# First block tile of the FFN: weight sums on VectorE, operands split behind T1 in buffers of their own, T4 behind them, GpSimd's sums behind T4

## The chip, the cores and the metric

The kernel runs on one core of one Trainium2 chip. The metric is the device time of one execution in microseconds (us), lower is better; the median of three runs stands for a kernel. All matrix products run on TensorE (PE); VectorE (DVE) and ScalarE (ACT) cast, subtract and apply nonlinearities; GpSimd (POOL) does some elementwise sums; SyncE (SP) issues the DMAs.

## The reference, cut to what matters

One decoder block: a normalised input goes through three mixers, a gated merge and an output projection, and then through a SwiGLU feed-forward net (FFN). Only the FFN's input side matters here. D_MODEL is 1024, D_FF is 2816, 1024 tokens.

```
u = rms_norm(h, norm_ffn[l])
gate_ff, up_ff = jnp.split(u @ w_ffn_in[l], 2, axis=-1)
h = h + (jax.nn.silu(gate_ff) * up_ff) @ w_ffn_out[l]
```

## The kernel before

**Precision by splitting.** Each fp32 operand is split into a high part (an ACT copy rounded to the matmul's format, line 118) and a low part (a DVE subtraction, line 119); `split` at line 115 issues the two. A product of split operands takes three matmuls for each 128 rows of the contraction: hi by hi, hi by lo, lo by hi (`mm3`, line 143).

**The FFN's input side.** The 22 tiles f of 128 FFN channels each need gate and up columns of the weights. They are taken as pairs j and j + 11 for j = 0 to 10. The pair j = 0 is computed plainly: `swiglu_plain` (line 919) for f = 0 and f = 11, four groups of 24 matmuls each (banks mm_g and mm_u). Its weights come through the pool wp (tags wr, wh, wl, two buffers each). All others go through `swiglu` (line 943), a 2 by 2 block scheme with seven products of 12 matmuls in place of eight. The weight blocks are a11, a12 (gate, two halves of the contraction) and a21, a22 (up). Sums on GpSimd make a21 := a11 - a21, s2 := a22 - a21, later a11 := a11 + s2 and a12 := a12 - s2. The products follow in this order, with the PSUM banks that the profile shows: a11 by b11 (mm_s), a12 by b21 (sc_s), s2 by T2 (mm_s, added), a11 + s2 by T1 (tr_s), a21 by T3 (mm_s, added), a12 - s2 by b22 (tr_s, added), a22 by T4 (mm_s, added). Between them ACT and DVE read the banks: g0 (ACT copy, line 952, then a DVE add of sc_s), g1 (ACT copy of mm_s after the third product, line 960), u1 (ACT copy of tr_s after the fourth, line 963; DVE add of mm_s after the fifth, line 965). A product that is added into a bank waits for the read before it: the sixth waits for u1's copy, the seventh for u1's add.

**The weight operands.** `operand` (line 914) splits one 512-wide block into a tile [128, 2, 512]. In `swiglu` the first and sixth product take theirs from wp under the tag wh (two buffers), the second and seventh under wl (two), the other three from the pool r5 under the tag ar (three). In the tags wh and wl the plain part's last weights lie until its last matmuls.

**The token operands.** `combine` (line 976) makes T1 to T4 from the four blocks of the normalised tokens, once: 18 DVE sums and differences over 1024 elements a row and eight pairs of ACT copy and DVE subtraction, T2 and T3 first, then T1, then T4 (two of each, for the two halves of the contraction). T4's share is four sums and two pairs. T4's tiles take the buffers that b12 leaves when the plain part's last matmuls on it are done; the sums' temporaries take four buffers under the tag fo.

**Sums for the output side.** `combine_w(j)` (line 1006) loads two tiles of the FFN's output weights under the tag fo and forms four sums on GpSimd; `combine_a(j)` (line 1022) forms four more on GpSimd from the results of the pair j and j + 11. Both store what they make to DRAM (bsp and asp), and nothing reads that until the output side begins at about 1444 us.

**The order.** In the loop (line 1035) j = 0 runs `swiglu_plain` twice, `combine`, `combine_w(0)` and `combine_a(0)`; j = 1 then fetches its weights and runs `swiglu(1)`, `swiglu(12)`, and so on. `fetch_fi(f, i)` (line 934) loads the weights of the first of a pair into wp's wr and of the second into r5's wr. A planner places each instruction ahead of the run: it walks the program with costs of its own, gives each engine at each time the earliest instruction in the program that it takes to be ready, and the engines then work off these queues strictly in order. So a queue's order is the planner's expectation, and an instruction that is late holds up all behind it on its engine.

Of the kernel before, what the change touches and what calls it, by code (L numbers as in the profile page):

```python
# [11 lines left out]
AF = mybir.ActivationFunctionType  # L12
ALU = mybir.AluOpType
# [33 lines left out]
def f32(ap):  # L47
    return ap.bitcast(F32)
# [3 lines left out]
def hybrid_block(ctx, tc, h_in, w_in, w_v0, w_v1, w_bd, par, rows, gains, relt, onehot,  # L52
                 maskrow, cmask, w_br, w_out, w_fi, w_fo, out):
    nc = tc.nc
    act, dve, pool, pe = nc.scalar, nc.vector, nc.gpsimd, nc.tensor
# [11 lines left out]
    wp = ctx.enter_context(tc.tile_pool(name="wstream", bufs=2, side="left"))  # L67
# [26 lines left out]
    warm = cp.tile([P, 1], F32, name="warm")  # L94
# [20 lines left out]
    def split(hi, lo, src, scale=None, pin=False):  # L115

        if scale is None:
            act.activation(hi, src, AF.Copy)  # L118
            i = dve.tensor_tensor(lo, src, f32(hi), ALU.subtract)  # L119
            if pin:  # L120
                tc.keep_in_program_order(i)
        else:
            act.activation(hi, src, AF.Copy, scale=scale)
            dve.scalar_tensor_tensor(lo, src, scale, f32(hi), ALU.mult, ALU.subtract)

    def load_w(src, n, pl=None, tag="w", bufs=None, lo_on_pool=False):
        pl = pl or wp
# [149 lines left out]
    with tc.tile_pool(name="r0", bufs=1, side="right", reuse_waits="tile") as r0:  # L277
# [68 lines left out]
        bb = r0.tile([P, 8, 383], F32, name="bb")  # L346
# [417 lines left out]
    def pair_tile(pl, **kw):  # L764

        return [pl.tile([P, D], F32R, tag="m4", name=nm("pt"), **kw).rearrange("p (k t) -> p k t", k=2)
                for a in range(2)]
# [32 lines left out]
    with tc.tile_pool(name="r3", bufs=16, side="right", reuse_waits="tile") as r3:  # L800
# [13 lines left out]
        ahead = [fetch(*x, r3) for x in todo[:2]]  # L814
# [80 lines left out]
    NJ = NF // 2  # L895
# [3 lines left out]
    def sub(eng, o, a, b):  # L899
        eng.tensor_tensor(o, a, b, ALU.subtract)  # L900

    def add(eng, o, a, b):
        eng.tensor_tensor(o, a, b, ALU.add)

    with tc.tile_pool(name="r5", bufs=1, side="right", reuse_waits="tile") as r5:
# [3 lines left out]
        def product(ps, a, b, first=True):  # L909

            run(mm3(ps, [(a[:, 0, k * P:(k + 1) * P], a[:, 1, k * P:(k + 1) * P],
                          b[k // 2][0][:, k % 2], b[k // 2][1][:, k % 2]) for k in range(4)], first))

        def operand(pl, tag, bufs, src):
            t = pl.tile([P, 2, 512], F32R, tag=tag, bufs=bufs, name=nm(tag))
            split(t[:, 0], t[:, 1], src)
            return t
# [16 lines left out]
        def fetch_fi(f, i):  # L934
            w = []
            for s in range(2):
                pl = r5 if i % 2 else wp
                raw = pl.tile([P, D], F32, tag="wr", bufs=2, name=nm("wr"))
                dma(raw, w_fi[f + NF * s])
                w.append(halves(raw))  # L940
            return w

        def swiglu(f, w, bb):

            (a11, a12), (a21, a22) = w
            b11, b21, b22, t1, t2, t3, t4 = bb
            p1, p2, p5 = mm_bank(f"_s{f}"), sc_bank(f"_s{f}"), tr_bank(f"_s{f}")
            g0, g1, u1 = (t5("c", 6) for _ in range(3))
            s0, s1 = (t5("a", 6) for _ in range(2))
            s2 = t5("s2", 2)  # L950
            product(p1, operand(wp, "wh", 2, a11), b11)
            act.activation(g0, p1, AF.Copy)  # L952
            product(p2, operand(wp, "wl", 2, a12), b21)
            add(dve, g0, p2, g0)
            act.activation(s0, g0, AF.Sigmoid)
            dve.tensor_tensor(s0, g0, s0, ALU.mult)
            sub(pool, a21, a11, a21)
            sub(pool, s2, a22, a21)
            product(p1, operand(r5, "ar", 3, s2), t2, False)
            act.activation(g1, p1, AF.Copy)  # L960
            add(pool, a11, s2, a11)
            product(p5, operand(r5, "ar", 3, a11), t1)
            act.activation(u1, p5, AF.Copy)
            product(p1, operand(r5, "ar", 3, a21), t3, False)
            add(dve, u1, p1, u1)
            sub(pool, a12, a12, s2)
            product(p5, operand(wp, "wh", 2, a12), b22, False)
            add(dve, g1, p5, g1)
            act.activation(s1, g1, AF.Sigmoid)
            dve.tensor_tensor(s1, g1, s1, ALU.mult)  # L970
            dve.tensor_tensor(s1, u1, s1, ALU.mult)
            product(p1, operand(wp, "wl", 2, a22), t4, False)
            dve.tensor_tensor(s0, p1, s0, ALU.mult)
            return [s0, s1]

        def combine():

            b11, b21 = u2[0][:2], u2[0][2:]
            b12, b22 = u2[1][:2], u2[1][2:]
            t3 = [pair_tile(r5, bufs=4) for _ in range(2)]  # L980
            t2, t1 = ([pair_tile(mp) for _ in range(2)] for _ in range(2))
            temp = lambda: t5("fo", 4, D).rearrange("p (k t) -> p k t", k=2)
            v2 = []
            for i in range(2):
                v3 = temp()
                v2.append(temp())
                for v, x, y in zip((v3, v2[i]), b22[i], b12[i]):
                    sub(dve, v, f32(x), f32(y))
                add(dve, v3, v3, v2[i])
                for x, y in zip((v3, v2[i]), b11[i]):  # L990
                    add(dve, v2[i], x, f32(y))
                split(*t2[i], v2[i])
                split(*t3[i], v3)
            t4 = [pair_tile(mp) for _ in range(2)]
            for t, b in ((t1, b22), (t4, b21)):
                for i in range(2):
                    v = temp()
                    sub(dve, v, f32(b[i][0]), v2[i])
                    add(dve, v, v, f32(b[i][1]))
                    split(*t[i], v)  # L1000
            return b11, b21, b22, t1, t2, t3, t4

        def spill(i, j, x):
            dma(asp[i][j], x)

        def combine_w(j):

            raws = []
            for i in range(2):
                raw = t5("fo", 4, D)  # L1010
                dma(raw, w_fo[(j + NJ * i) * P:(j + NJ * i + 1) * P])
                raws += halves(raw)
            b11, b12, b21, b22 = raws
            t2 = zp.tile([P, 512], F32, tag="z", bufs=2, name=nm("t2"))
            sub(pool, b12, b22, b12)
            add(pool, t2, b12, b11)
            sub(pool, b11, b22, t2)
            sub(pool, b21, b21, t2)
            for i, x in ((2, t2), (3, b11), (4, b12), (6, b21)):
                dma(bsp[i][j], x)  # L1020
# [14 lines left out]
        for j in range(NJ):  # L1035
            if j == 0:
                first, second = swiglu_plain(0), swiglu_plain(NJ)
                bb = combine()
                spill(0, j, first[0])
            else:  # L1040
                first = swiglu(j, fetch_fi(j, 0), bb)
                spill(0, j, first[0])
                second = swiglu(j + NJ, fetch_fi(j + NJ, 1), bb)
            combine_w(j)
            combine_a(j, *first, *second)
    ctx4.close()


# [173 lines left out]
```

## Time and profile before

| | us |
|---|---|
| median of three runs | 1662.85 (1662.39 to 1664.62) |
| the profiled execution's own time | 1662.29 |
| its span, first to last instruction | 1660.5 |
| PE busy | 1630.2 (98%) |
| DVE busy | 999.4 (60%) |
| ACT busy | 760.7 (46%) |
| POOL busy | 433.1 (26%) |

The span is counted from the first instruction. Busy shares are averages over stages; what bounds a stage has to be read in that stage. PEclk is the granted TensorE clock, 1.00 for full speed. In the timeline a row is one engine's run of like instructions: start, length, what it does, and in brackets the idle time before it with what ended it.

### The profile page before, as it was taken

What the parts mean: (1) busy time and instruction counts of PE and PEld (TensorE: products, weight loads), DVE (VectorE), ACT (ScalarE), POOL (GpSimd) and SP (SyncE); (2) the same over time, 40 slices, a digit from 0 to 9 for tenths busy, and PEclk for the clock granted to TensorE, in tenths of its full rate; (3) what the DMA queues carried; (4) which work ended last, traced back from release to release, by engine and by line L of the source; (5) the groups of instructions that cost most, each with busy time, mean ns of one, the idle gap of its engine ahead of it and who ended that gap; (6) DMA issues with size and microseconds to landing.
All of it is one profiled execution on the core that took longest, in us unless ns stands there. A gap on an engine that the chain in (4) does not pass through costs nothing.

```text
span 1660.5 us, 22597 instructions
## 1 busy us (share of the span) xinstructions
PE 1630.2 (98%) x8159; PEld 1375.1 (83%) x8159; DVE 999.4 (60%) x1799; ACT 760.7 (46%) x1397; POOL 433.1 (26%) x341
## 2 busy tenths in 40 slices
PE   7999999999999999999999999899999999999998
PEld 6898978888888888888887888688888888888886
DVE  6565556555566666641348437977666676567544
ACT  6456466555555555542336434333333333345342
POOL 2111001001122221110225001776666566300000
PEclk9999999999999999999999999899999999999999
DMA  7132352223324142339737221464444443598642
GB/s 255 63 108 93 122 153 79 88 89 121 108 76 129 59 122 79 107 114 320 244 127 235 102 77 70 158 222 169 165 147 146 146 161 131 197 356 278 195 128 101
DMA packets 110879, 242.47 MB, mean 146 GB/s; under 512 B 11944, under 2 KB 23544, under 8 KB 110512
## 3 DMA queue, kind: packets, MB, share of 16 engines
q1 hardware_dynamic: 110768, 241.04, 42.7%
q8 instruction: 64, 1.05, 0.3%
q14 instruction: 47, 0.39, 0.1%
HBM read 163.45 MB, written 72.21 MB: 142 GB/s over the span
## 4 chain that ended last, share of the span: by engine, by line
PE 87%; DVE 4%; issue 4%; ACT 2%; POOL 1%; DMA 1%; SPq 0%; DVEq 0%; POOLq 0%; ACTq 0%
PE mm_w L150 26%; PE mm_s L150 13%; PE tr_s L150 7%; PE mm_br L150 6%; PE mm_wo L150 5%; PE mm_x L1086 4%; PE tr_y L1086 4%; PE sc_y L1086 4%; PE ob L547 3%; PE sc_s L150 3%; PE tr L558 3%; PE mm_v L150 2%; PE ob_x L1086 1%; PE mm_g L150 1%; PE mm_u L150 1%
## 5 line engine op out<-in xcount | busy, mean ns | idle before, releaser
L150 PE MATMUL mm_w<-uh,wh 128*128 128x512 f32 (+2 forms) x744 | 292.6, 393 | 0.0
L150 PE MATMUL mm_w<-uh,wl 128*128 128x512 f32 (+2 forms) x744 | 280.5, 377 | 0.0
L150 PE MATMUL mm_w<-ul,wh 128*128 128x512 f32 (+2 forms) x744 | 279.9, 376 | 0.0
L150 PEld LDWEIGHTS mm_w<-uh,wl 128*128 128x128 f32 x744 | 140.0, 188 | 25.7
L150 PEld LDWEIGHTS mm_w<-uh,wh 128*128 128x128 f32 x744 | 140.4, 189 | 12.7
L150 PEld LDWEIGHTS mm_w<-ul,wh 128*128 128x128 f32 x744 | 140.7, 189 | 11.7
L119 DVE TENSOR_TENSOR ab<-raw,ab 128x1024 fp32r<-128x1024 f32 x77 | 93.0, 1224 | 71.6 <-ACT ab L118 69.6
L118 ACT ACTIVATE ab<-raw 128x1024 fp32r<-128x1024 f32 x77 | 80.9, 1059 | 94.7 <-PE ob_x L1086 23.4
L150 PE MATMUL mm_s<-pt,ar 128*128 128x512 f32 x480 | 117.4, 394 | 3.7 <-ACT c L952 3.7
L118 ACT ACTIVATE wh<-wr 128x1024 fp32r<-128x1024 f32 (+1 forms) x85 | 72.7, 856 | 103.2 <-PE mm_w L150 50.6
L150 PE MATMUL mm_br<-o,wh 128*128 128x512 f32 x384 | 118.3, 389 | 0.0
L119 DVE TENSOR_TENSOR pl<-tr,ph 128x384 fp32r<-128x384 f32 (+2 forms) x160 | 87.4, 555 | 47.0 <-ACT ph L118 43.1
L150 PEld LDWEIGHTS mm_s<-pt,ar 128*128 128x128 f32 x480 | 91.5, 191 | 23.6 <-ACT c L952 4.5
L118 ACT ACTIVATE ph<-tr 128x384 fp32r<-128x384 f32 (+2 forms) x160 | 76.8, 485 | 53.6 <-PE tr L558 51.5
L119 DVE TENSOR_TENSOR wl<-wr,wh 128x1024 fp32r<-128x1024 f32 x45 | 55.6, 1235 | 72.2 <-ACT wh L118 71.9
L648 POOL TENSOR_SCALAR s<-s,sm 128x144 f32<-128x144 f32 (+3 forms) x64 | 48.6, 761 | 172.1 <-DVE sm L647 144.2
L150 PEld LDWEIGHTS mm_br<-o,wh 128*128 128x128 f32 x384 | 72.1, 188 | 14.9
L558 PE MATMUL tr<-ident,s 128*128 128x128 f32 x480 | 79.6, 274 | 1.2 <-POOL s L596 0.6
L150 PE MATMUL mm_wo<-woh,hl 128*128 128x512 f32 x256 | 79.1, 390 | 0.0
L150 PE MATMUL mm_br<-o,wl 128*128 128x512 f32 x192 | 75.3, 392 | 1.5 <-DVE wl L119 1.4
L558 PEld LDWEIGHTS tr<-ident,s 128*128 128x128 f32 x480 | 59.1, 140 | 18.3 <-DVE pl L119 3.4
L1086 PE MATMUL mm_x<-ab 128*128 128x512 f32 x297 | 72.7, 389 | 0.0
(252 smaller groups left out, 3687.9 us busy)
## 6 DMA issues: line engine op xcount, KB each, us to landing
wr<-w_in_dram SPq DMA_DIRECT2D x45, 512.0 KB, 3.7
wr<-w_fi_dram SPq DMA_DIRECT2D x44, 512.0 KB, 3.8
raw<-asp SPq DMA_DIRECT2D x77, 256.0 KB, 3.2
asp<-a SPq DMA_DIRECT2D x66, 256.0 KB, 2.5
gz<-z SPq DMA_DIRECT2D x48, 256.0 KB, 2.1
o<-osp SPq DMA_DIRECT2D x24, 512.0 KB, 6.1
sg<-gz SPq DMA_DIRECT2D x48, 256.0 KB, 3.2
fo<-w_fo_dram SPq DMA_DIRECT2D x22, 512.0 KB, 5.1
```

The costliest lines, as they stand in the source:

```text
L118: act.activation(hi, src, AF.Copy)
L119: i = dve.tensor_tensor(lo, src, f32(hi), ALU.subtract)
L150: pe.matmul(ps, a, b, start=first and i == 0, stop=i == n - 1, skip_group_check=not first)
L547: pe.matmul(ob[:, q0:q0 + b - a], vt[:, c], x[:, a:b], start=count == 0, stop=count == n_mm - 1, skip_group_check=True)
L558: pe.transpose(tb[:, col:col + P], src, ident)
L648: pool.tensor_scalar(s[:, :nk], s[:, :nk], den, 1.0, ALU.mult, ALU.mult)
L1086: pe.matmul(banks[x], a[:, 0, q], b[:, 1], start=first and j == 0 and c == 0, stop=j == NJ - 1 and c % 3 == 2, skip_group_check=True)
```

## The change

- `split` returns its two instructions.
- `fetch_fi` swaps the pools: the first of a pair goes to r5's wr, the second to wp's wr.
- `combine` stops after T1 and returns T1's last two split instructions (ACT's and DVE's) and a function `rest` that makes T4.
- At j = 0, behind `combine`, the weights of f = 1 are fetched and `swiglu(1)` is written there, with all of its ACT and DVE instructions queued behind T1's last split. In it a11, a12 and s2 are split first, into the three ar buffers; the sums a21 and s2 on DVE stand between; then T4 is made; then the products follow. All four weight sums of f = 1 are on DVE.
- A one-element GpSimd copy `seen` reads T4's last low part. The GpSimd instructions of `combine_w`, `combine_a` and of the second `swiglu` of each pair are queued behind it.
- For f = 12 (j = 1) the sums a21 and s2 are on DVE as well; its other two stay on GpSimd. All later tiles are as before.

```diff
         def fetch_fi(f, i):
...
-                pl = r5 if i % 2 else wp
+                pl = wp if i % 2 else r5
...
-        def swiglu(f, w, bb):
+        def swiglu(f, w, bb, eng, later=None):
...
+            def s32():
+                sub(eng[0], a21, a11, a21)
+                sub(eng[0], s2, a22, a21)
+
+            if later is None:
+                t4 = bb[6]
+                o1, o2 = (lambda: operand(wp, "wh", 2, a11)), (lambda: operand(wp, "wl", 2, a12))
+            else:
+
+                x1, x2 = (operand(r5, "ar", 3, a) for a in (a11, a12))
+                s32()
+                x3 = operand(r5, "ar", 3, s2)
+                t4 = later()
+                o1, o2 = (lambda: x1), (lambda: x2)
+            product(p1, o1(), b11)
...
-            sub(pool, a21, a11, a21)
-            sub(pool, s2, a22, a21)
-            product(p1, operand(r5, "ar", 3, s2), t2, False)
+            if later is None:
+                s32()
+                x3 = operand(r5, "ar", 3, s2)
+            product(p1, x3, t2, False)
...
-            add(pool, a11, s2, a11)
+            add(eng[1], a11, s2, a11)
...
-            sub(pool, a12, a12, s2)
+            sub(eng[1], a12, a12, s2)
...
+            last = less_t2(t1, b22)
+
+            def rest():
+                t4 = [pair_tile(mp) for _ in range(2)]
+                less_t2(t4, b21)
+                return t4
+            return [b11, b21, b22, t1, t2, t3], last, rest
...
-                bb = combine()
+                bb, last, rest = combine()
                 spill(0, j, first[0])
+                w = fetch_fi(1, 0)
+                with tc.issue_after(last[0]), tc.issue_after(last[1]):
+                    ahead = swiglu(1, w, bb, (dve, dve), lambda: bb.append(rest()) or bb[6])
+
+                seen = pool.tensor_copy(warm[:, 0:1], f32(bb[6][1][1][:, 0, :1]))
             else:
-                first = swiglu(j, fetch_fi(j, 0), bb)
+                first = ahead if j == 1 else swiglu(j, fetch_fi(j, 0), bb, (pool, pool))
                 spill(0, j, first[0])
-                second = swiglu(j + NJ, fetch_fi(j + NJ, 1), bb)
-            combine_w(j)
-            combine_a(j, *first, *second)
+                with tc.issue_after(seen.ins):
+                    second = swiglu(j + NJ, fetch_fi(j + NJ, 1), bb, (dve if j == 1 else pool, pool))
+            with tc.issue_after(seen.ins):
+                combine_w(j)
+                combine_a(j, *first, *second)
```

## Rows read from the trace of the kernel before

**Rows 1.** The page's share of busy time in 40 equal slices of the span (41.5 us each), in tenths.
```profile
PE   7999999999999999999999999899999999999998
DVE  6565556555566666641348437977666676567544
```
**Rows 2.** Busy time by stretch (columns: stretch in us, its length, then busy us and instructions of PE, PEld, DVE, ACT, POOL, then PEclk, DMA share, GB/s), from the start of the token sums to past the first block tile.
```profile
1013.00:1052.80 39.80, 39.80 (x177) 32.95 (x176) 39.11 (x39) 16.07 (x23) 14.27 (x5) 1.00 0.22 73
1052.80:1060.00 7.20, 4.28 (x18) 2.92 (x17) 7.20 (x7) 2.73 (x4) 5.43 (x3) 1.00 0.46 146
1060.00:1066.00 6.00, 2.94 (x9) 1.80 (x7) 4.37 (x4) 0.48 (x1) 5.92 (x5) 0.55 0.57 218
1066.00:1072.00 6.00, 5.32 (x15) 4.24 (x16) 5.82 (x5) 2.41 (x6) 5.29 (x4) 0.59 0.41 142
```
**Rows 3.** Timeline of PE over the first block tile, f = 1: the plain part's end and the products with b11, b21, T2, T1, T3.
```profile
1052.82 0.61 PE L150 MATMUL mm_s<-pt,wh 128*128 128x512 f32 x2
1054.33 2.56 PE L150 MATMUL mm_s<-pt,wh 128*128 128x512 f32 x10 [0.90 <-DVE wh L119]
...
1059.37 3.57 PE L150 MATMUL sc_s<-pt,wl 128*128 128x512 f32 x10 [2.02 <-DVE wl L119]
1066.68 4.96 PE L150 MATMUL mm_s<-pt,ar 128*128 128x512 f32 x12 [3.75 <-ACT c L952]
1071.48 2.88 PE L150 MATMUL tr_s<-pt,ar 128*128 128x512 f32 x12
1074.20 2.88 PE L150 MATMUL mm_s<-pt,ar 128*128 128x512 f32 x12
```
**Rows 4.** PE's waits from 1050 to 1440 us, all of them (columns: who waited for whom, total us, times, longest).
```profile
PE mm_s L150 <- ACT c L952: 3.7, 1, 3.7
PE sc_s L150 <- DVE wl L119: 2.0, 1, 2.0
PE mm_s L150 <- DVE wh L119: 0.9, 1, 0.9
```
**Rows 5.** The same columns as rows 2 in steps of 1 us: where the granted clock falls and where it rises again.
```profile
1060.00:1061.00 1.00, 1.00 (x5) 0.80 (x4) 1.00 (x2) 0.00 (x0) 0.92 (x2) 0.82 0.00 0
...
1070.00:1071.00 1.00, 1.00 (x4) 0.79 (x3) 1.00 (x2) 0.00 (x0) 0.37 (x2) 0.56 0.05 20
```
**Rows 6.** Timeline of ACT.
```profile
1048.66 0.64 ACT L118 ACTIVATE ar<-s 128x512 fp32r<-128x512 f32 x1 [9.69 <-POOL s L900]
...
1065.52 0.63 ACT L118 ACTIVATE wh<-wr 128x512 fp32r<-128x512 f32 x1 [7.25 <-POOL wr L900]
1066.05 0.58 ACT L952 ACTIVATE c<-mm_s 128x512 f32<-128x512 f32 x1
...
1072.28 0.62 ACT L118 ACTIVATE ar<-s 128x512 fp32r<-128x512 f32 x1
1074.40 0.60 ACT L963 ACTIVATE c<-tr_s 128x512 f32<-128x512 f32 x1 [1.50 <-PE tr_s L150]
```
**Rows 7.** Timeline of DVE: the token sums, T1 and T4, then the weights of f = 1 and f = 12 (an operation over 1024 elements a row is full width, over 512 half width).
```profile
1015.52 2.29 DVE L900 TENSOR_TENSOR fo<-pt,pt 128x1024 f32<-128x1024 f32 x1
...
1039.52 1.73 DVE L119 TENSOR_TENSOR pt<-fo,pt 128x1024 fp32r<-128x1024 f32 x1
1041.17 2.35 DVE L900 TENSOR_TENSOR fo<-pt,fo 128x1024 f32<-128x1024 f32 x2
...
1044.04 3.44 DVE L903 TENSOR_TENSOR fo<-fo,pt 128x1024 f32<-128x1024 f32 x2
1047.40 2.31 DVE L900 TENSOR_TENSOR fo<-pt,fo 128x1024 f32<-128x1024 f32 x1
1050.28 1.67 DVE L119 TENSOR_TENSOR pt<-fo,pt 128x1024 fp32r<-128x1024 f32 x1 [0.57 <-ACT pt L118]
...
1053.60 0.68 DVE L119 TENSOR_TENSOR wh<-wr,wh 128x512 fp32r<-128x512 f32 x1
...
1057.57 1.75 DVE L119 TENSOR_TENSOR wl<-wr,wl 128x512 fp32r<-128x512 f32 x1
...
1070.55 0.68 DVE L903 TENSOR_TENSOR c<-sc_s,c 128x512 f32<-128x512 f32 x1
...
1073.08 1.78 DVE L119 TENSOR_TENSOR ar<-s,ar 128x512 fp32r<-128x512 f32 x1
...
1077.12 0.69 DVE L903 TENSOR_TENSOR c<-mm_s,c 128x512 f32<-128x512 f32 x1 [0.56 <-PE mm_s L150]
```
**Rows 8.** Timeline of POOL: a sum with little beside it, then the first and the ninth of an almost unbroken run of sums (seven more lie between them).
```profile
1015.44 1.29 POOL L900 TENSOR_TENSOR wr<-wr,wr 128x512 f32<-128x512 f32 x1 [98.09 <-DVE pt L124]
...
1056.52 2.25 POOL L900 TENSOR_TENSOR fo<-fo,fo 128x512 f32<-128x512 f32 x1
...
1070.71 1.30 POOL L903 TENSOR_TENSOR wr<-s,wr 128x512 f32<-128x512 f32 x1 [0.63 <-DVE wh L119]
```
**Rows 9.** SP's queue: issues of DMAs in order.
```profile
1009.54 2.81 SPq L58 DMA_DIRECT2D wr<-w_fi_dram  x2
...
1040.19 0.33 SPq L58 DMA_DIRECT2D asp<-a  x1
1040.56 0.43 SPq L58 DMA_DIRECT2D wr<-w_fi_dram  x1
```

More of the change, by code (lines that the diff above doesn't have):

```diff
@@ L117, in split @@
         if scale is None:
-            act.activation(hi, src, AF.Copy)
+            a = act.activation(hi, src, AF.Copy)
             i = dve.tensor_tensor(lo, src, f32(hi), ALU.subtract)
@@ L122, in split @@
         else:
-            act.activation(hi, src, AF.Copy, scale=scale)
-            dve.scalar_tensor_tensor(lo, src, scale, f32(hi), ALU.mult, ALU.subtract)
+            a = act.activation(hi, src, AF.Copy, scale=scale)
+            i = dve.scalar_tensor_tensor(lo, src, scale, f32(hi), ALU.mult, ALU.subtract)
+        return a.ins, i.ins
     def load_w(src, n, pl=None, tag="w", bufs=None, lo_on_pool=False):
@@ L941, in fetch_fi @@
             return w
-        def swiglu(f, w, bb):
+        def swiglu(f, w, bb, eng, later=None):
             (a11, a12), (a21, a22) = w
-            b11, b21, b22, t1, t2, t3, t4 = bb
             p1, p2, p5 = mm_bank(f"_s{f}"), sc_bank(f"_s{f}"), tr_bank(f"_s{f}")
@@ L950, in swiglu @@
             s2 = t5("s2", 2)
-            product(p1, operand(wp, "wh", 2, a11), b11)
+            b11, b21, b22, t1, t2, t3 = bb[:6]
+            def s32():
[11 more added lines that the diff above has]
+            product(p1, o1(), b11)
             act.activation(g0, p1, AF.Copy)
-            product(p2, operand(wp, "wl", 2, a12), b21)
+            product(p2, o2(), b21)
             add(dve, g0, p2, g0)
@@ L993, in combine, with less_t2 @@
                 split(*t3[i], v3)
-            t4 = [pair_tile(mp) for _ in range(2)]
-            for t, b in ((t1, b22), (t4, b21)):
+            def less_t2(t, b):
                 for i in range(2):
@@ L999, in combine @@
                     add(dve, v, v, f32(b[i][1]))
-                    split(*t[i], v)
-            return b11, b21, b22, t1, t2, t3, t4
+                    last = split(*t[i], v)
+                return last
+            last = less_t2(t1, b22)
[4 more added lines that the diff above has]
+            return [b11, b21, b22, t1, t2, t3], last, rest
         def spill(i, j, x):
```

## The prediction

> **What bounds the kernel now.** First the page's slices of busy time: PE is at nine tenths or more in all but the first and last slices and one in the middle, around 1040 to 1080 us, and there DVE is at nine [rows 1]. So PE is the bound, and the one place where it loses time is where the FFN's token sums and first block tile fall. Then the stretches: up to 1052.8 PE is fully busy and DVE nearly so (39.11 of 39.80 us); in the next 13 us PE is busy for only 4.28 of 7.20 and 2.94 of 6.00 us, and the granted clock drops to about half [rows 2]. PE's timeline shows the loss. The plain part ends and the first product starts at 1052.82; a product takes 2.72 us from start to start (1071.48 to 1074.20), so T1's, the fourth, should start at 1052.82 + 3 x 2.72 = 1060.98. It starts at 1071.48 [rows 3]. **10.5 us** are lost, and no product after it is late: the list of waits holds 0.9, 2.0 and 3.7 us and nothing else until 1440 [rows 4]. The other 3.8 us are matmuls at the lower level, 1.2 GHz: the clock falls at about 1060.6, after the first two waits, and is back at 2.4 GHz at about 1070.9, some 4 us after work resumed [rows 5]; ten matmuls take 3.57 us and twelve 4.96 in place of 2.88 [rows 3]. The gain can't pass 10.5 us, 0.63%.
>
> Who is late? DVE splits a11 and a12 late (the first two waits), because T4 and the rest of the sums stand before them. The third wait is for ACT's g0 copy, and ACT stood 7.25 us behind a split that waited for a GpSimd sum [rows 6]. DVE is slow besides: a full-width operation, 1.22 us in an undisturbed run (2.35 for two), takes 2.31 while GpSimd sums run; a half-width one takes 0.68 alone and 1.75 to 1.78 beside GpSimd; one that reads PSUM stays at 0.68 there [rows 7].
>
> **The change part by part.** *T1 earlier.* T1's last low part ends at about 1051.9 now. Three of T4's operations before it go behind it: 3 x 1.13 (from start to start) = 3.4 us. GpSimd is silent until T4 is done, so these excesses go: 2.29 - 1.22, 1.73 - 1.22, 3.44 - 2.35, 2.31 - 1.22, 1.67 - 1.22 and the 0.57 of idling, together 4.8 [rows 7]. In their place DVE waits once for ACT's copy of T1's last sum, about 1.1. T1 ends at 1051.9 - 3.4 - 4.8 + 1.1 = 1044.8.
>
> *Operands and T4.* Then DVE does, alone, five half-width operations (low parts of a11, a12, s2, two sums) at 0.60 from start to start, two of the plain part's multiplications (1.2) and T4's six of 1.13: 3.0 + 1.2 + 6.8 = 11.0, so T4 ends at **1055.8**. The operands of the first three products are ready by about 1050, before PE needs them at 1052.82, even if T1 came 2 us late. They lie in ar, so they need no buffer of the plain part; T4 is first read by the seventh product, 16.3 us after 1052.82. The 0.9 and 2.0 us waits and the clock's first fall go, and I cost this part at nothing on the path.
>
> *Weights.* The tiles of f = 1 come into r5's buffers, whose loads are issued at 1009.54 now; wp's second load was issued at 1040.56, right behind a store of a GpSimd result [rows 9]. That store moves behind T4, so f = 12's loads, now in wp, no longer stand behind it. Nothing is lost.
>
> *GpSimd's queue.* Behind T4 stand `seen`, the four sums of `combine_w(0)`, the four of `combine_a(0)` and then f = 12's remaining two. Now they begin at 1056.52 and eight take 1070.71 - 0.63 - 1056.52 = 13.6 us, 1.70 each [rows 8]. They begin about when they do now, at 1057, so the eight end at 1070.6, while PE is 10.5 us ahead. Their stores on SP move with them, and the loads behind these (f = 2's weights, 13 us or more ahead of need) have slack.
>
> *What is late next.* DVE takes over six sums, 0.60 each. From 1055.8 its queue holds, ahead of f = 12's s2 becoming ready: two sums and two low parts for a11 and a12, low parts of a22 and a21, two operations for the gate, two low parts of f = 12, its sums a21 and s2, twelve in all, 12 x 0.60 = 7.2. GpSimd's eight sums fall into just this time. In rows 7, from 1057.57 to the one at 1073.08, ten half-width operations from SBUF take 14.8 us, 1.48 each or 0.8 more than 0.68, beside about ten GpSimd sums. So 8 x 0.8 = 6.4 us come on top: s2 of f = 12 is ready at 1055.8 + 7.2 + 6.4 = 1069.4. The planner, which counts no such excess (it let ACT run into that 7.25 us wait), expects it at about 1063 and will put its ACT copy ahead of u1's, as it stands now (1072.28 before 1074.40 [rows 6]). So u1's copy ends at 1069.4 + 0.62 + 0.60 = 1070.6, and the sixth product, due at 1052.82 + 5 x 2.72 = 1066.42, waits **4.2 us**. A wait of that size is likely to bring the lower clock back: the bounds are nothing and the whole 3.3 us of its present cost (1.2 and 2.1 by rows 3); I take the 2.1 of the one full product, being the nearest case of work after a long wait. The same backlog holds u1's add in DVE's queue, where f = 12's low parts stand before it as now (1073.08 before 1077.12), which this wait covers.
>
> Sum: 10.5 - 4.2 - 2.1 = **4.2 us** gained. The profiled execution's 1662.29 (span 1660.5 and 1.8 around it) would become 1658.1; it lies 0.6 below the median, so the median becomes 1662.85 - 4.2 = **1658.7**. Bounds of the excess for one GpSimd sum: nothing gives no wait (1652.4); 1.1, the most that rows 7 show (1.78 - 0.68), gives 8.8 in place of 6.4, a wait of 6.6 and with the clock's 3.3 a gain of 0.6 (1662.3).
>
> **The rivals.** *No new stall.* If the planner puts f = 12's DVE and ACT work behind u1's copy and add, or the excess is small, PE runs through: 1662.85 - 10.5 = 1652.4. For it: since 1074 the same engines serve PE without a wait, with GpSimd beside them. Against it: the orders named above.
>
> *Full exclusion.* If each GpSimd sum holds DVE off for its whole 1.29 us [rows 8], eight cost 10.3: s2 at 1073.3, the sixth product at 1074.5, a wait of 8.1 and 2.1 for the clock, a gain of 0.3: 1662.6. Against it, no row shows over 1.1. This is the Trainium skill's rule (SBUF — State Buffer, section "Who interferes with whom"): the two engines share a port pair under an exclusive lock, and a VectorE operation with two SBUF inputs contends with GpSimd's reads. The rule speaks against gathering GpSimd's sums where DVE has most to do; the trace agrees in kind (0.68 for PSUM sources, up to 1.78 for SBUF) but shows less than a whole sum's length.
>
> *Slower: GpSimd's queue.* f = 12's sum a11 + s2 stands in GpSimd's queue behind whatever the planner thought ready first. If it expects the eight sums done before s2, it puts sums of `combine_w(1)` in the gap. With four of them a11 + s2 ends at 1070.6 + 5 x 1.70 = 1079.1; its ACT copy and low part stand before u1's add (0.62 + 0.69 + 0.69), so the seventh product, due at 1069.14, starts at 1081.1: 12.0 lost, 14.1 with the clock, 3.6 more than now: 1666.4. It turns from gain to loss at two such sums. For it: the planner takes GpSimd to be faster than it is; against it: those sums need their own load first.
>
> **How the numbers follow.** Forecast 0.45; no new stall 0.22; full exclusion 0.17; slower 0.16. What a measurement can tell from no change is 0.2%, 3.3 us. The forecast's own range, 1653 to 1662.3, puts about 0.30 of its 0.45 beyond that; with the 0.22 faster has 0.52. Full exclusion, the forecast's rest and the slower case with two or three sums make 0.36 the same; 0.12 is left for slower. The range 1652.2 to 1664.5 leaves out the slower case's upper part.
>
> **What would show it.** Right: the first five products 2.72 us apart from about 1052.8; T4's last low part near 1056 and GpSimd's first sum just after; one PE wait of 3 to 7 us at f = 1's sixth or seventh product, released by ACT's u1 copy or DVE's add, with an ACT copy of s2 (or of a11) just before it; PEclk near 0.5 in the products after it; f = 12 without waits. Wrong: PE late for x1 or x2 (T1 later than I work out), no wait at all, or a wait after f = 1, where I expect none because GpSimd catches up in its idle time.

## The result and the profile after

| | before | after |
|---|---|---|
| median, us (11 runs each, same chip) | 1662.39 (1660.84 to 1664.62) | 1665.34 (1664.79 to 1667.67) |
| ratio, 95% interval | | 1.002 (1.0012 to 1.0028) |
| profiled execution, us | 1662.29 | 1667.67 |
| its span, us | 1660.5 | 1665.9 |
| f = 1's first product starts, us | 1052.82 | 1054.13 |
| from there to the start of f = 12's second product | 32.26 | 36.20 |

The change makes the kernel slower by 2.95 us, 0.18%; the interval lies wholly on the slow side. The time lies outside the range of the prediction.

Of the 5.4 us between the two profiled executions, 1.3 lie ahead of f = 1: the plain part ends later. In the fourteen executions profiled for this study f = 1 starts anywhere between 1051.65 and 1054.66 us, behind the same plain part, so this 1.3 is taken as scatter and not as an effect of the change. From f = 1's first product to f = 12's second, eight products lie; at 2.72 us each they need 21.76 us. Before they took 32.26, that is 10.5 lost; now they take 36.20, **14.4 lost**. The difference is 3.9 us, inside the interval of the ratio (2.0 to 4.7 us).

The two views that tell where: first the waits of PE in the profile after, between 1000 and 1440 us (columns as in [rows 4]). The three of before are gone, and two others are there.

```profile
PE mm_s L151 <- DVE c L904: 4.9, 1, 4.9
PE tr_s L151 <- ACT c L980: 3.7, 1, 3.7
```

Then PE's timeline after, from f = 1's first product on (it answers to [rows 3]):

```profile
1054.13 2.88 PE L151 MATMUL mm_s<-pt,ar 128*128 128x512 f32 x12
1056.85 2.88 PE L151 MATMUL sc_s<-pt,ar 128*128 128x512 f32 x12
...
1065.01 2.88 PE L151 MATMUL mm_s<-pt,ar 128*128 128x512 f32 x12
1071.54 5.49 PE L151 MATMUL tr_s<-pt,wh 128*128 128x512 f32 x12 [3.65 <-ACT c L980]
1081.91 5.49 PE L151 MATMUL mm_s<-pt,wl 128*128 128x512 f32 x12 [4.87 <-DVE c L904]
1087.19 3.30 PE L151 MATMUL mm_s<-pt,wh 128*128 128x512 f32 x12
1090.33 2.88 PE L151 MATMUL sc_s<-pt,wl 128*128 128x512 f32 x12
```

The first five products stand 2.72 us apart: what the change was to remove, it removed. Then the sixth waits 3.65 us for u1's copy (ACT, line 980), and the seventh another 4.87 us for u1's add (DVE, line 904). Each of the two takes 5.49 us in place of 2.88, and the one after them 3.30. Waits 8.5, matmuls at the lower clock 2.6 + 2.6 + 0.4 = 5.6: that is the 14.4, to 0.3 (a wait is counted from the end of the product before it, 0.16 after the next one could have started).

Who is late for the sixth? Timeline of DVE after, from T4's last part on (compare [rows 7]):

```profile
1056.47 0.68 DVE L904 TENSOR_TENSOR wr<-s,wr 128x512 f32<-128x512 f32 x1
1057.07 0.69 DVE L901 TENSOR_TENSOR wr<-wr,s 128x512 f32<-128x512 f32 x1
1057.68 1.23 DVE L119 TENSOR_TENSOR pt<-fo,pt 128x1024 fp32r<-128x1024 f32 x1
...
1061.74 1.78 DVE L119 TENSOR_TENSOR wl<-wr,wl 128x512 fp32r<-128x512 f32 x1
1063.44 1.77 DVE L972 TENSOR_TENSOR a<-c,a 128x512 f32<-128x512 f32 x1
1065.14 1.78 DVE L119 TENSOR_TENSOR wh<-wr,wh 128x512 fp32r<-128x512 f32 x1
...
1068.54 1.75 DVE L901 TENSOR_TENSOR s<-wr 128x512 f32<-128x512 f32 x1
1071.04 0.92 DVE L119 TENSOR_TENSOR ar<-s,ar 128x512 fp32r<-128x512 f32 x1 [0.76 <-ACT ar L118]
1080.17 1.08 DVE L119 TENSOR_TENSOR ar<-wr,ar 128x512 fp32r<-128x512 f32 x1 [8.21 <-ACT ar L118]
1081.18 0.68 DVE L904 TENSOR_TENSOR c<-mm_s,c 128x512 f32<-128x512 f32 x1
```

T4 is done at 1058.9. Up to there a half-width operation takes 0.68; beside GpSimd's sums it takes 1.75 to 1.78, 1.70 from start to start. So f = 12's s2 (1068.54) is ready at 1070.3 only. Two lines of ACT's timeline after show what hangs on it, and a third on what the seventh's wait hangs:

```profile
1070.38 0.63 ACT L118 ACTIVATE ar<-s 128x512 fp32r<-128x512 f32 x1 [7.29 <-DVE s L901]
1070.91 0.58 ACT L980 ACTIVATE c<-tr_s 128x512 f32<-128x512 f32 x1
1079.51 1.15 ACT L118 ACTIVATE ar<-wr 128x512 fp32r<-128x512 f32 x2 [8.02 <-POOL wr L904]
```

ACT idles 7.29 us before its copy of s2, which DVE has not made yet; u1's copy is next in its queue, though the fourth product, which it reads, ended at 1065.2. Later ACT idles 8.02 us before its copy of f = 12's a11 + s2, which GpSimd (POOL) has not made. DVE idles 8.21 us for that copy, to make its low part; u1's add, for which PE waits, comes after it, though u1's copy was done at 1071.5. POOL's timeline after shows why a11 + s2 is late:

```profile
1059.51 1.76 POOL L901 TENSOR_TENSOR fo<-fo,fo 128x512 f32<-128x512 f32 x1
...
1071.37 1.72 POOL L901 TENSOR_TENSOR a<-a,t 128x512 f32<-128x512 f32 x1
1073.05 1.27 POOL L901 TENSOR_TENSOR fo<-fo,fo 128x512 f32<-128x512 f32 x1
1074.40 1.28 POOL L904 TENSOR_TENSOR t<-fo 128x512 f32<-128x512 f32 x1
1075.76 2.50 POOL L901 TENSOR_TENSOR fo<-fo,t 128x512 f32<-128x512 f32 x2
1078.21 1.26 POOL L904 TENSOR_TENSOR wr<-s,wr 128x512 f32<-128x512 f32 x1
```

The eight sums of j = 0, which like those of `combine_w(1)` have no haste (nothing reads them before the output side), fill it from 1059.51 to 1073.05. Then come the four of `combine_w(1)` (1073.05 to 1078.21, the one with x2 is two), and only then a11 + s2, done at 1079.5. Its source s2 was there from 1070.3, so it could have begun at 1073.05.

Last, stretches of the profile after (columns as in [rows 2]): PE's clock.

```profile
1072.00:1074.00 2.00, 2.00 (x6) 1.54 (x6) 0.00 (x0) 0.00 (x0) 2.00 (x2) 0.50 0.70 270
1082.00:1084.00 2.00, 2.00 (x5) 1.61 (x6) 1.90 (x4) 0.63 (x1) 0.00 (x0) 0.50 0.46 182
1088.00:1089.00 1.00, 1.00 (x6) 0.80 (x5) 0.79 (x2) 0.06 (x1) 0.80 (x1) 1.00 0.03 10
```

After each of the two waits the granted clock is 0.50, that is 1.2 GHz, though PE is busy throughout; at 1088 it is back at 1.00.

### The profile page after: what moved, and what is told of

Its sections match the earlier page's. It is cut to its first block, busy times and chain, and to the rows that moved or that the text cites. A ratio compares the mean times of both kernels' runs of the same rounds, so it can differ in the third digit from the quotient of the medians.

```text
span 1665.9 us, 22589 instructions
## 1 busy us (share of the span) xinstructions
PE 1632.4 (98%) x8159; PEld 1376.9 (83%) x8159; DVE 993.3 (60%) x1805; ACT 761.4 (46%) x1397; POOL 415.3 (25%) x336
## 4 chain that ended last, share of the span: by engine, by line
PE 84%; DVE 5%; issue 4%; ACT 2%; DMA 2%; POOL 2%; SPq 0%; DVEq 0%; POOLq 0%; ACTq 0%
PE mm_w L151 24%; PE mm_s L151 13%; PE tr_s L151 6%; PE mm_br L151 6%; PE mm_wo L151 5%; PE mm_x L1118 4%; PE tr_y L1118 4%; PE sc_y L1118 4%; PE ob L548 3%; PE sc_s L151 3%; PE tr L559 3%; PE mm_v L151 2%; PE ob_x L1118 1%; PE mm_g L151 1%; PE sc L633 1%
```

## The experiments

The theory after the result: GpSimd's sums, gathered behind T4, make DVE late (first wait) and then keep f = 12's a11 + s2 behind sums that have no haste (second wait); the orders of ACT's and DVE's queues pass both on to PE. The rivals: that DVE is simply overloaded by the sums it took over; that the waits would only move when the order is mended. Every edit below is one to the changed kernel. Since the start of f = 1 scatters by 3 us, the table also has the time from f = 1's first product to the end, as the profiled execution's time less that product's start.

| kernel | median, us (runs) | ratio to before, interval | profiled: f = 1 to the end |
|---|---|---|---|
| before | 1662.39 (11) | | 609.5 |
| the change | 1665.34 (11) | 1.002 (1.0012 to 1.0028) | 613.5 |
| e1_w1_behind | 1659.21 (11) | 0.9983 (0.9975 to 0.9992) | 606.9 |
| e2_f12_dve | 1659.22 (11) | 0.9981 (0.9972 to 0.999) | 606.3 |
| e3_u1_first | 1658.74 (11) | 0.9976 (0.9967 to 0.9985) | 606.5 |
| e6_both | 1658.28 (11) | 0.9976 (0.9967 to 0.9984) | 606.5 |
| e4_no_sums0 | 1652.03 (5) | 0.994 (0.9928 to 0.9953) | 599.0 |
| e5_no_seen | 1660.3 (11) | 0.999 (0.9981 to 0.9999) | 607.3 |
| e8_hold | 1663.84 (11) | 1.0008 (0.9999 to 1.0017) | 611.0 |
| e9_f12_first | 1659.89 (11) | 0.9986 (0.9977 to 0.9995) | 607.1 |
| e7_f12_pool | 1663.4 (10) | 1.0007 (0.9998 to 1.0016) | 610.3 |
| e10_w_later | 1656.8 (5) | 0.9964 (0.9951 to 0.9976) | 602.9 |
| e11_w_later2 | 1668.6 (5) | 1.0037 (1.0024 to 1.0051) | 613.8 |
| e12_w_catch_up | 1657.78 (7) | 0.9972 (0.9961 to 0.9983) | 604.2 |

Each ratio is to runs of before taken beside that kernel on the same chip; their medians lie between 1662.18 and 1662.85, and "below before" means below these. The change was not run again beside the experiments, so a difference to its 1665.34 is one between chips and carries that scatter of some 0.7 us.

**The sums of j = 1 behind f = 12's** (e1_w1_behind). `add` and `sub` return their instruction here and below.

```diff
-            sub(eng[1], a12, a12, s2)
+            tail[f] = sub(eng[1], a12, a12, s2).ins
...
-            with tc.issue_after(seen.ins):
+            with tc.issue_after(tail[NJ + 1] if j == 1 else seen.ins):
                 combine_w(j)
                 combine_a(j, *first, *second)
```

> The changed kernel, but the GpSimd sums of j = 1 (combine_w(1), combine_a(1)) are queued behind f = 12's last weight sum, so its a11 + s2 stands ninth behind T4 and not thirteenth. Theory (GpSimd's queue makes the second wait): a11 + s2 ends at about 1074.4 in place of 1079.5, its ACT copy and low part by 1075.7, u1's add by 1076.4, before the sixth product ends at about 1077; the wait of 4.9 us before the seventh product goes, the 3.7 us before the sixth stays. 4.9 to 7.5 us under the changed kernel (the upper end if the clock is back at 2.4 GHz for the seventh product): 1657.8 to 1660.5. Rival (DVE has too much work in this stretch, by the sums moved to it): u1's add is as late as before, both waits stay, 1665.

Measured 1659.21, as the theory had it: 6.1 below the change. PE's timeline of this kernel, sixth and seventh product:

```profile
1071.79 5.48 PE L151 MATMUL tr_s<-pt,wh 128*128 128x512 f32 x12 [3.65 <-ACT c L980]
1077.08 3.00 PE L151 MATMUL mm_s<-pt,wl 128*128 128x512 f32 x12
```

The sixth's wait stays at 3.65, the seventh's is gone, and with it the second fall of the clock. So four sums without haste, ahead of f = 12's a11 + s2 in GpSimd's queue, make the second wait, and all of it.

**All of f = 12's sums on DVE** (e2_f12_dve).

```diff
-                    second = swiglu(j + NJ, fetch_fi(j + NJ, 1), bb, (dve if j == 1 else pool, pool))
+                    second = swiglu(j + NJ, fetch_fi(j + NJ, 1), bb, (dve, dve) if j == 1 else (pool, pool))
```

> The changed kernel, but all four weight sums of f = 12 are on DVE, two more there. Theory (GpSimd's queue makes the second wait): a11 + s2 follows s2 on DVE at about 1070.3, u1's add is done by 1074 to 1075, the wait before the seventh product goes, the one before the sixth stays at 3 to 5 us: 1657.5 to 1660.5. Rival (too much work on DVE): two more operations of up to 1.78 us each make both waits longer, 1666 to 1669.

Measured 1659.22. The first wait is 3.6; of the second 1.5 are left, behind sums that DVE now makes itself. It agrees with e1 on the place: two sums more on DVE are cheaper than two behind GpSimd's backlog, so DVE's own load is not the cause of the second wait.

**u1's copy and add ahead of f = 12's late work** (e3_u1_first). f = 12's sums a21 and s2 and the splits of s2 and a11 + s2 are queued behind f = 1's u1 copy and add.

```diff
+            if f == NJ + 1:
+                for x in u1s[1]:
+                    behind.enter_context(tc.issue_after(x))
...
-            act.activation(u1, p5, AF.Copy)
+            u1s[f] = [act.activation(u1, p5, AF.Copy).ins]
```

> The changed kernel, but f = 12's sums a21 and s2 and the splits of s2 and a11 + s2 are queued behind f = 1's u1 copy on ACT and u1 add on DVE. GpSimd's order stays. Theory (both waits are the work of f = 12 standing ahead of f = 1's in strictly ordered queues): no wait in f = 1. GpSimd's a11 + s2 still ends near 1079.5, and ACT's copy of it now stands ahead of f = 12's g0 copy, so f = 12's third product, due near 1078.6, waits 3 to 4 us, with some 2 us for the clock: 1656.5 to 1659. Rival (the buffers: the three ar tiles taken by the early operands hold up the later ones whatever the order): waits stay in f = 1, 1662 or more.

Measured 1658.74. Both waits of f = 1 are gone; one came back in f = 12, at its third product, in PE's list of waits of this kernel:

```profile
PE mm_s L151 <- ACT c L968: 4.4, 1, 4.4
```

It is the size expected (3 to 4), 0.4 over. Line 968 is g0's copy: ACT is again behind a split whose source is late. So the orders pass the lateness on, and mending them at one place moves it.

**Both** (e6_both): the edits of e1 and e3 together.

> e3's order on ACT and DVE and e1's on GpSimd together. Theory: f = 12's s2 is split by about 1073.5 and a11 + s2 by about 1076, before PE needs them (1078.6 and 1081.3), and f = 1 runs through, so PE has no wait after 1054: all of the changed kernel's 14 us of waits and low clock go, 1651 to 1652.5, which is 10 to 11 us under the kernel before. Rival (too much work on DVE and GpSimd in this stretch, whatever the order): the waits come back in f = 12, 1657 or more.

Measured 1658.28: a miss by 6 us, and the rival was right. Three views of this kernel, PE, ACT and DVE:

```profile
1086.47 5.49 PE L151 MATMUL mm_s<-pt,ar 128*128 128x512 f32 x12 [4.27 <-ACT c L982]
```

```profile
1085.31 0.63 ACT L971 ACTIVATE a<-c 128x512 f32<-128x512 f32 x1 [7.87 <-DVE c L904]
1085.84 0.58 ACT L982 ACTIVATE c<-mm_s 128x512 f32<-128x512 f32 x1
```

```profile
1082.93 1.75 DVE L119 TENSOR_TENSOR wh<-wr,wh 128x512 fp32r<-128x512 f32 x1
1084.60 0.68 DVE L904 TENSOR_TENSOR c<-sc_s,c 128x512 f32<-128x512 f32 x1
```

The wait stands two products further, at f = 12's fifth. ACT waits 7.87 us for g0's add, which DVE reaches only at 1084.60, with operations of 1.75 us ahead of it. DVE is still late, because GpSimd is still at its sums.

**Without the eight sums of j = 0** (e4_no_sums0). This is the test of the root: what `combine_w(0)` and `combine_a(0)` store is stored unsummed, so the kernel leaves out that part of the FFN's result. Their loads and stores stay.

```diff
-            sub(pool, b12, b22, b12)
...
+            if j == 0:
+                t2 = b22
+            else:
+                sub(pool, b12, b22, b12)
...
+            if j == 0:
+                s2 = a22
+            else:
+                sub(pool, a21, a11, a21)
```

> The changed kernel without the eight GpSimd sums of j = 0: combine_w(0) and combine_a(0) store their inputs as they are in place of the sums (that part of the FFN's result is left out). DVE's and ACT's work stays. Theory (GpSimd's sums slow DVE): f = 12's half-width operations on DVE take 0.68 us in place of 1.75, its s2 is ready near 1064 in place of 1070.3, and GpSimd has nothing ahead of a11 + s2: neither wait of the changed kernel is left, 1651 to 1653. Rival (DVE has too much work there by the six sums moved to it): the wait before the sixth product stays at 2 us or more, and the clock's loss with it, 1656 or more.

Measured 1652.03, 10.2 us below before, within the theory's range. PE's list of waits is empty from 1000 to 1440. In DVE's timeline of this kernel the operations that took 1.75 to 1.78 are back at 0.68:

```profile
1061.72 0.68 DVE L119 TENSOR_TENSOR wh<-wr,wh 128x512 fp32r<-128x512 f32 x1
...
1062.92 0.68 DVE L901 TENSOR_TENSOR s<-wr 128x512 f32<-128x512 f32 x1
```

From f = 1 to the end it takes 599.0 us: the 609.5 of before less the 10.5 that before loses there. So DVE with all six moved sums is in time, s2 is ready at 1063.6 in place of 1070.3, and both waits hang on the eight sums of GpSimd. The rival of a DVE overloaded by what it took over falls, and so does one that the trace would also allow, that DVE is slowed by the transfers beside it: from 1060 to 1064, where its operations take 0.68 here, the DMA engines move 356 GB/s, and in the change, where they take 1.75 to 1.78 (1060.6 to 1070.3), 122.

**Without the hold** (e5_no_seen): `seen` and the queueing behind it are left out, so GpSimd may begin ahead of T4's end.

```diff
-                seen = pool.tensor_copy(warm[:, 0:1], f32(bb[6][1][1][:, 0, :1]))
...
-            with tc.issue_after(seen.ins):
+            if True:
```

> The changed kernel without its last part: GpSimd's sums are not held behind T4 (no copy seen). In GpSimd's queue f = 12's a11 + s2 then stands behind the eight sums of j = 0 and ahead of those of j = 1. Theory: the sums start some 3 us earlier and slow T4 a little, which has slack; the wait before the seventh product goes, the one before the sixth stays at 2 to 4 us: 1656.5 to 1660. Rival (holding GpSimd back is what keeps T4 and the first operands in time): a wait before the first or the seventh product by T4, 1662 or more.

Measured 1660.3, 5.0 below the change and 0.3 over the theory's upper end. PE waits 0.9 at the fifth product and 4.4 at the sixth, and not at the seventh. In POOL's timeline f = 12's a11 + s2 now stands ahead of the sums of j = 1:

```profile
1067.48 1.71 POOL L901 TENSOR_TENSOR a<-a,t 128x512 f32<-128x512 f32 x1
1071.07 1.27 POOL L904 TENSOR_TENSOR wr<-s,wr 128x512 f32<-128x512 f32 x1 [1.88 <-issue]
```

So the part of the change that holds GpSimd behind T4 costs 5 us by itself: without it one of the eight sums is done before 1035 and the other seven begin at 1056.88, the order in the queue is another, and the second wait does not come.

**GpSimd held a second time** (e8_hold): e6, and all later GpSimd work held until f = 12's g0 is there.

```diff
+            if j == 1:
+                with tc.issue_after(tail[NJ + 1]):
+                    seen = pool.tensor_copy(warm[:, 0:1], gs[NJ + 1][:, :1])
```

> e6 (f = 12's work behind f = 1's u1, GpSimd's sums of j = 1 behind f = 12's), and the GpSimd sums of j = 1 and of f = 2 are held back further, behind a small copy that reads f = 12's g0 after its add. Theory (DVE is only slow beside GpSimd): between f = 12's last GpSimd sum and g0's add DVE's half-width operations take 0.68 us in place of 1.75, g0's add is done near 1077 in place of 1085 and the wait that e6 has left (4.3 us before f = 12's fifth product) goes: 1651 to 1653. Rival (there is more work than the engines can do here; a wait only moves): the wait comes up again in f = 12 or in f = 2, 1656 or more.

Measured 1663.84, a miss by 11 us. e6's wait is gone, as meant, but PE and ACT of this kernel show the next one:

```profile
1090.98 4.71 PE L151 MATMUL tr_s<-pt,wh 128*128 128x512 f32 x12 [5.25 <-ACT c L991]
...
1117.52 4.61 PE L151 MATMUL mm_s<-pt,wl 128*128 128x512 f32 x12 [2.79 <-DVE c L904]
```

```profile
1089.81 0.63 ACT L118 ACTIVATE ar<-s 128x512 fp32r<-128x512 f32 x1 [8.62 <-POOL s L901]
```

The products with brackets are f = 12's sixth and f = 2's seventh. Now the sums of f = 2, which are GpSimd's, are late: ACT waits 8.62 for f = 2's s2, and f = 12's u1 copy, for which the sixth waits, is next in its queue. The time in which GpSimd is kept still is missing afterwards. The wait of 2.79 is of the same kind as the change's second: f = 2's u1 add stands on DVE behind the low part of f = 13's a11 + s2, which GpSimd makes only from 1113.81 to 1115.09.

**f = 12's two sums first** (e9_f12_first): behind T4 first f = 12's two, then the sums of j = 0 and j = 1.

```diff
+            if j == 0:
+                first0, second0 = first, second
+                continue
+            with tc.issue_after(tail[NJ + 1]):
+                if j == 1:
+                    combine_w(0)
+                    combine_a(0, *first0, *second0)
```

> The changed kernel, with f = 12's two GpSimd sums first behind T4 and the sums of j = 0, then of j = 1, behind them. GpSimd then has nothing to do until f = 12's s2 is ready on DVE. Theory (GpSimd beside DVE, and GpSimd's order): s2 is ready near 1064, a11 + s2 near 1065.5, no wait in f = 1; the eight sums then fall beside f = 1's end and f = 12, where at most 1 to 3 us of wait come up: 1651.5 to 1656. Rival (the same amount of contention, only moved, costs the same): waits of 4 us or more in f = 12, with the clock, 1657 or more.

Measured 1659.89, above the theory's range and in the rival's. No product of f = 1 waits, and f = 12's s2 is ready at 1063.6 as in e4, though the eight sums are only moved here. f = 12's seventh waits:

```profile
1093.77 4.60 PE L151 MATMUL mm_s<-pt,wl 128*128 128x512 f32 x12 [4.80 <-DVE c L904]
```

ACT stands 5.52 us behind f = 2's a11 + s2 (1090.08 to 1091.34 on GpSimd), which has the eight, five sums of j = 1 and f = 2's own two ahead of it: the wait is the change's second one, one tile later. f = 2's seventh waits another 1.0.

**f = 12's a21 and s2 back on GpSimd** (e7_f12_pool).

```diff
-                    second = swiglu(j + NJ, fetch_fi(j + NJ, 1), bb, (dve if j == 1 else pool, pool))
+                    second = swiglu(j + NJ, fetch_fi(j + NJ, 1), bb, (pool, pool))
```

> The changed kernel with f = 12's sums a21 and s2 back on GpSimd; the rest of the change stays. Theory: s2 stands behind the eight sums of j = 0 and one of j = 1 in GpSimd's queue and ends near 1076 in place of 1070.3, so the wait before the sixth product grows from 3.7 to 9 us or so; a11 + s2 follows two sums later, near 1079, so the wait before the seventh product shrinks to 1 to 3 us: 1664 to 1669. Rival (the sums moved to DVE are what costs): without them the wait before the sixth product shrinks, 1661 or less.

Measured 1663.4, just under the theory's range, with one wait of 8.7 us at the sixth product (9 expected) and none at the seventh. In PE's timeline:

```profile
1075.53 5.04 PE L151 MATMUL tr_s<-pt,wh 128*128 128x512 f32 x12 [8.75 <-ACT c L980]
1080.41 2.92 PE L151 MATMUL mm_s<-pt,wl 128*128 128x512 f32 x12
```

Here the first wait does cover the second: a11 + s2 is done at 1077.2 and u1's add at 1079.6, while the sixth product runs. Two sums of f = 12 on DVE bring nothing as the change stands, which by the medians is 1.9 us slower with them: one wait of 8.7 is about as long as the two of 3.7 and 4.9, and costs the clock once.

**The output's weight sums one pair later** (e10_w_later): e9, and `combine_w(j - 1)` behind `combine_a(j)` in place of `combine_w(j)` ahead of it, so that GpSimd has four sums fewer at the place.

```diff
+                if j == 1:
+                    combine_a(0, *first0, *second0)
...
+                combine_w(j - 1)
+                if j == NJ - 1:
+                    combine_w(j)
```

> e9 (f = 12's two GpSimd sums first behind T4), and each pair's combine_w, four GpSimd sums that nothing needs before the output side, comes one pair later. Theory (e9's waits came from f = 2's GpSimd sums standing behind those of j = 0 and j = 1): between f = 12's sums and f = 2's s2 only five others are left where e9 has nine, f = 2's s2 ends near 1079 in place of 1084.7 and its a11 + s2 near 1084 in place of 1091.3, just when they are used; no PE wait over 1 us: 1651.5 to 1654, which is 8 to 11 us under the kernel before. Rival (GpSimd's and DVE's work here is more than there is room for, a wait only moves): a wait of 3 us or more comes up in f = 2 or f = 13, 1656 or more.

Measured 1656.8, the lowest median here of a kernel that computes everything: 5.4 below before, 8.5 below the change (e12's interval overlaps it). No product of the FFN's input side waits. The theory's upper end was 1654; what it left out comes at the end of the FFN. SP's queue of this kernel there (columns as in [rows 9]):

```profile
1441.33 0.42 SPq L58 DMA_DIRECT2D bsp<-t  x1
1441.81 0.95 SPq L58 DMA_DIRECT2D bsp<-fo  x2
1442.86 0.40 SPq L58 DMA_DIRECT2D bsp<-t  x1
1443.69 1.56 SPq L58 DMA_DIRECT2D bsp<-fo  x2
1445.31 0.42 SPq L58 DMA_DIRECT2D raw<-w_fo_dram  x1
```

The stores of the postponed sums (bsp) stand ahead of loads of the output side (raw), which ACT then waits for, and PE for ACT (in e4 the first of these loads goes out at 1440.40):

```profile
PE mm_x L1127 <- ACT ab L118: 1.1, 1, 1.1
PE sc_y L1127 <- DVE ab L119: 0.6, 1, 0.6
...
```

With 0.3 and 0.2 more these are all of PE's waits from 1050 us on, 2.2 us. From f = 1 to the end it takes 602.9, 3.9 more than e4; the input side (until the output's first product, 1432.98) takes 381.3 against e4's 380.8, so 3.4 of the 3.9 lie in the output side. The waits are 2.2 of that; the rest was not followed.

**Two pairs later, and caught up in time** (e11_w_later2, e12_w_catch_up): `combine_w(j - 2)` with the rest at the last pair; and e10 with two `combine_w` at j = 5, so that nothing is left for the end.

```diff
+                if j > 1:
+                    combine_w(j - 2)
+                if j == NJ - 1:
+                    combine_w(j - 1)
+                    combine_w(j)
```

```diff
+                if j <= 5:
+                    combine_w(j - 1)
+                if j == 5:
+                    combine_w(j)
```

> As e10, with combine_w two pairs later. Theory: four sums between f = 12's and f = 2's s2, the same or a little better than e10, 1651.5 to 1653.5. Rival (the wait moves on): 1656 or more; or, since the last pairs' sums now all fall to the end of this stage, a wait where the output side reads them.

> As e10, but combine_w is one pair late only up to j = 5, where two pairs' sums are done; from j = 6 on it stands in its own pair again. Theory (e10's 2.2 us of waits at the start of the output side come from the last pairs' sums and stores falling late): they go, and no wait comes in their place in the FFN's input side as GpSimd has idle time in each pair: 1651.5 to 1654. Rival (GpSimd has no room for four sums more in any pair without an operand being late): a wait of 2 us or more near 1240 to 1280, 1655 or more.

Measured 1668.6 and 1657.78. With eight sums left for the end the output side waits 9.4 us in e11, 5.3 of it at once, and the time is the worst of all. With the catching up these waits are gone, but two are in the middle, in PE's timeline of e12:

```profile
1296.07 3.02 PE L151 MATMUL mm_s<-pt,ar 128*128 128x512 f32 x12 [1.25 <-ACT c L977]
1304.17 3.01 PE L151 MATMUL mm_s<-pt,wl 128*128 128x512 f32 x12 [2.37 <-DVE c L904]
```

The pair into which the four sums more were put had no room for them there either. In both, the rival was right (in e12 the waits come a little later than its 1240 to 1280).

## Why the prediction was wrong

**What it had right.** T1 came in time (its last low part ended at 1046.5; 1044.8 and the later start of this execution, 1.3, give 1046.1), and PE went through the first five products (forecast: 2.72 apart). T4 ended at 1058.9; 1055.8 + 1.3 gives 1057.1. The 1.8 in between are three sums that the forecast had behind T4 and that stand ahead of its last part, at 0.60 each: f = 1's a11 + s2 and a12 - s2 (1056.47 and 1057.07) and f = 12's a21 (1042.29). s2 was ready at 1070.3, forecast 1069.4 + 1.3 = 1070.7. The excess by which DVE was slowed was 5 x 1.1 + 0.5 = 6.0 us, forecast 6.4. That these are so close is partly luck: the forecast took 0.8 for each of eight sums, and it was 1.1 for each operation that ran beside one, but of these there were only six, the first for half its length. ACT's copy of s2 stood ahead of u1's copy, and the sixth product waited 3.65, forecast 4.2. The 10.5 us were there to be had: e4 got all of them.

**The step that failed** is the sentence on u1's add: that f = 12's low parts stand before it, "which this wait covers". The sixth's wait did not cover it. One of these low parts is that of a11 + s2, and its source was GpSimd's, done at 1079.5, that is 8 us after the sixth product had begun. The prediction had the mechanism as its slower rival, with its parts (four sums of `combine_w(1)` in the gap, a11 + s2 done at 1079.1, the seventh product at 1081.1, 14.1 lost; measured 1079.5, 1081.9 and 14.4), and gave it 0.16. That its times fit to 0.8 us is luck in part: the eight sums ended 2.5 us later than it had them, and the five sums behind them, with DVE idle beside them, took 6.4 us in place of 8.5. What it held against it, that these sums need their own load first, was no obstacle: the first of them begins at 1073.05, right behind the eighth sum, with no idle time ahead of it. And it treated forecast and rival as either or. They are two waits on two queues, and both came, one behind the other: the sixth's from DVE's slowness, the seventh's from GpSimd's order. e1 shows them apart: it takes the second away and leaves the first at 3.65. The lateness does not add up, though. The seventh product was due at 1054.13 + 6 x 2.72 = 1070.45 and started 11.5 us later, when a11 + s2 allowed it; the sixth's wait and its slow matmuls lie within these 11.5. By these rows the seventh would have started no earlier with the sixth in time, so GpSimd's queue set the loss. That is worked out and not shown, as no run takes away the first wait alone.

**A term that was mis-sized** is the clock. The forecast took 2.1 us, for one product at 1.2 GHz. There were two, each behind a wait, and they cost 2.6 + 2.6 and 0.4 of the next. With the measured terms the forecast's sum is 10.5 - 3.65 - 4.87 - 5.6 = -3.6, and the medians differ by -2.95.

**Full exclusion**, the rival at 1662.6, was not what decided, but its price for one sum, 1.29, was nearer to the 1.1 measured than the forecast's 0.8. While both engines work without a break, DVE's operations and GpSimd's sums start every 1.70 us, one of each; alone they start every 0.60 and 1.22 (POOL, 1078.21 to 1079.43 in the profile after, with DVE idle), 1.82 in sum. The Trainium skill (SBUF — State Buffer, section "Who interferes with whom") says that a VectorE operation with two SBUF inputs contends with a GpSimd operation that reads there, and that the contention is an exclusive lock. The trace comes within 0.12 us of that, for operations of this size: 1.1 us per DVE operation, and GpSimd's sum goes from 1.27 to 1.74.

**The cause**, then, is eight GpSimd sums without haste, gathered where DVE has its most urgent work (shown by e4, which leaves them out): they slow DVE, which makes the first wait, and they leave GpSimd late, so that four more sums ahead of a11 + s2 make the second (shown by e1). The orders of the queues decide where the lateness comes out and how much of it: at f = 1's sixth and seventh product in the change, f = 12's third in e3, its fifth in e6, its seventh in e9, f = 12's sixth and f = 2's seventh in e8, the output side in e10 and e11, the middle of the FFN in e12. Against the change, order alone brought 1.5 to 7.1 us (e1, e3, e5, e6, e8, e9), putting `combine_w` one pair later 8.5 (e10), and two pairs later cost 3.3 (e11).

**What stays open.** Whether another spreading of the 88 sums gets from e10's 1656.8 nearer to e4's 1652.0; the five that were tried (e8 to e12) each found a new wait. And the scatter of the plain part's end, 3 us over the profiled executions, lies ahead of the change and was not followed.

## What to carry to other kernels

When a stall is taken away, follow every queue that feeds the next few steps to its end, and for each step take the latest of its sources: a wait covers another only if that one's source is ready by then, and where two engines are late the later one sets the loss. On engines that work off their queues in order, ask of each late instruction what without haste stands ahead of it. Work moved out of the way of one stage falls into another; price it there, with the slowing of its neighbour, before counting the gain.

## What the runs showed of the hardware

- DVE and GpSimd in step: with sums from SBUF on both, each engine starts one operation every 1.70 us (DVE 1061.74, 1063.44, 1065.14 in the change; alone 0.60), to within 0.01 us. An operation of DVE that reads PSUM is not held (0.68 at 1084.60 in e6, right behind one of 1.75, with a GpSimd sum running from 1084.09 to 1085.80).
- After waits of 2.79 to 8.75 us a product of twelve matmuls took 4.60 to 5.49 us in place of 2.88, at a granted clock of 0.50 for most of it (the change, e1 to e3, e5 to e9). After waits of 0.89 to 2.37 (e2, e5, e9, e12) it took 3.01 to 3.03, at 1.00. In the kernel before, the waits of 0.90 and 2.02 [rows 3] were followed by a clock of 0.55 [rows 2]. The longer waits cost 1.7 to 2.6 us more than themselves, and up to 0.4 in the product behind; the longest, 8.75, did not cost the most (2.2).
